# Nine instead of four gate units among the second block's mixers, with room from a smaller descriptor ring, shared masks and a borrowed slot

## The chip, the cores and the metric

The kernel runs on one core of one Trainium2 chip. The metric is device microseconds (us) of one execution. Besides the time, each kernel has one profiled execution, from which every row below is taken. Engines are PE (matrix multiply), DVE (vector), ACT (scalar, tables), POOL (GpSimd) and SP, which issues the weight loads.

## The reference

Two transformer blocks on 256 tokens with a model width of 2048, all in float32. The first block has two mixers (sparse attention, RWKV) and a mixture of experts. The second, which the change is about, is:

```python
proj  = rmsnorm(x, g) @ w_in                    # 2048 -> 12288 columns
gates = sigmoid(proj[..., o_c:].reshape(bsz, seq, 3, 2048) + b_gate)
y_a = gmlp_mixer(proj[..., :2048], ...)         # u * (tril(W) v + b)
y_b = s5_mixer(proj[..., 2048:3072], ...)       # complex diagonal recurrence over time,
                                                # then gelu, then g * sigmoid(g @ w_glu + b)
y_c = stick_breaking_attention(q, k, v)         # 8 heads
br  = einsum('blnw,nwd->blnd', [y_a, y_b, y_c], w_branch)
x = x + sum(gates * br, over the 3 branches) @ w_out
x = x + square(relu(rmsnorm(x) @ w_mlp_in)) @ w_mlp_out
```

## The kernel before

**Weights.** Every dense product is made in two pieces. A 512 KB chunk of weights (`raw`) is loaded by SP, ACT copies its rounded part to `wh` (L213), DVE subtracts to get the rest, `wl` (L214), and PE multiplies both with the activations (L223). One chunk of `w_in` in the second block is 24 matmuls of 256 columns. Both `wh` and `wl` come from a pool of three buffers each, so ACT and DVE can be at most three chunks ahead of PE.

**A gate unit.** `gate` (L1505) makes 256 of the 6144 gate columns: four chunks, so 96 matmuls, four `wh`, four `wl`, then one DVE multiplication by the norm's factors (L1510) and two ACT sigmoids (L1515). There are 24 units. Four of them (`EARLY`) are made among the mixers and kept in the pool `ge`; the other 20 are made one by one in `branch`, each beside the branch product that uses it. Work is the same wherever a unit is made; only its neighbours differ.

**The order in block 2.** `block2` walks `ORDER2`, a list of the dense units: `U` (gMLP), `C` (inputs of S5), `W` (gMLP values), `V` and `Q` (attention), `G` (gate units), `GM`, and `E` (the gelu of S5's output). After each step of a unit a nominal time of PE is added to a count, and each time the count passes `RS`, one step of S5 is written down (`states`: L1989 to L2029). S5 has 32 scans, each a chain on DVE (`a`, L1989 to L1992, and four L2002 scans), then POOL (`b`, `z`, L2004 and L2005; `sl`, L2017), ACT (`sh`) and PE. What the loops write down is then put in order by a scheduler, so that each engine's final order is not the written one.

**Sigmoids.** Their table differs from the ones that the attention heads (`zsb`, `zsc`, up to Exp) and gelu use. So the sigmoids of early units are held back (`held`) until the gelu; one unit's are let go there, the rest in `glu`.

**After the mixers** come `glu` (its input split is `gs`), the `w_branch` products with the remaining gate units, `w_out`, and the MLP.

**Parameter rows.** `late_params` (L449) is called at the start of `moe`, before its slots for weights (`own`, `ring`) are made. It loads 128 rows of 128 parameters by seven DMAs of POOL into a tile, transposes that on PE (L181), and copies the result to `parl`, which the router of the experts needs as `g_ffn` and block 2 as `b_gate` and others. The tile is one of its own, `parl_r`. `cst_c` names the tiles of constants.

Of the kernel before, what the change touches and what calls it, by code (L numbers as in the profile page):

```python
# [10 lines left out]
F32 = mybir.dt.float32  # L11
# [3 lines left out]
OP = mybir.AluOpType  # L15
# [13 lines left out]
def _consts():  # L29
    p = np.arange(128)[:, None]  # L30
    f = np.arange(128)[None, :]
    t = np.arange(T)[None, :]
    c = {}
    c["ident"] = p == f
    c["bd64"] = (p // 64) == (f // 64)
    for d in (128, 64):
        half = d // 2
        inv = np.float32(10000.0) ** (-np.arange(half, dtype=np.float32) * np.float32(2.0 / d))
        ang = np.arange(T, dtype=np.float32)[:, None] * inv.astype(np.float32)[None, :]
        cos = np.cos(ang).astype(np.float32).T  # L40
        sin = np.sin(ang).astype(np.float32).T
        c[f"cos{d}"] = np.tile(cos, (128 // half, 1))
        c[f"sin{d}"] = np.tile(np.concatenate([-sin, sin], 0), (128 // d, 1))
    c["m01"] = np.concatenate([p < 64, p >= 64], 1)
    s, u = p % 64, f[:, :64]
    c["gmask"] = np.concatenate([(s < u) & (p < 64), (s < u) & (p >= 64), s <= u], 1)
    lv = []
    for l in range(6):
        b = 1 << l
        lv.append(((p // (2 * b)) == (f // (2 * b))) & ((p // b) % 2 == 0) & ((f // b) % 2 == 1))  # L50
    c["lev"] = np.concatenate(lv[LB:], 1)
    b = 1 << LB
    c["blk"] = (p // b) == (f // b)
    c["nsel"] = np.where(p % b == f[:, :b], -1.0, 0.0)
    c["iota"] = np.broadcast_to(f, (128, 128))
    c["before"] = p < f
    c["geq"] = p >= f
    c["strict"] = p < f
    c["tril"] = p >= f
    c["ntril"] = np.where(p >= f, -1.0e30, 0.0)  # L60
    c["half"] = (p // 64) == np.arange(2)[None, :]
    c["odd"] = (p // 16) % 2 == np.arange(2)[None, :]
    c["tidx"] = np.broadcast_to(t.astype(np.float32), (128, T))
    return {k: np.ascontiguousarray(v, dtype=np.float32) for k, v in c.items()}
# [3 lines left out]
C1 = ("bd64", "cos128", "sin128", "cos64", "sin64", "m01",  # L68
      "gmask", "lev", "blk", "nsel")
C2 = ("iota", "before")  # L70
C3 = ("geq", "strict", "tril", "ntril", "half", "odd")


def const_arrays():
# [41 lines left out]
class Ker:  # L116
# [47 lines left out]
            return self.mx.tile([128, 512], F32, name="mx", tag="side", bufs=1)  # L164
        return self.mx.tile([128, 512], F32, name="mx", tag="mx", bufs=3)

    def param_rows(self, items, pool, name, q=None):
        nc = self.nc
        n = sum(i[2] for i in items)
        assert n <= 128  # L170
        r = pool.tile([128, 128], F32, name=name + "_r", tag="prow")
        nc.vector.memset(r, 0.0)
        o, where = 0, {}
        for key, parts, cnt in items:
            for ap, r0, c0 in parts:
                rr, cc = ap.shape
                self.tc.keep_in_program_order((q or nc.gpsimd).dma_start(r[o + r0:o + r0 + rr, c0:c0 + cc], ap))
            where[key] = (o, o + cnt)
            o += cnt
        ps = self.pmx()  # L180
        nc.tensor.transpose(ps[:, :128], r, self.ident)  # L181
        p = pool.tile([128, 128], F32, name=name)
        nc.vector.tensor_copy(p, ps[:, :128])
        return {k: p[:, a:b] for k, (a, b) in where.items()}
# [263 lines left out]

    def late_params(self):  # L449

        A = self.A
        row = lambda n: A[n].rearrange("l (r c) -> (l r) c", c=128)
        self.par = self.param_rows([
            ("g_ffn", [(row("g_ffn"), 0, 0)], 16), ("norm1", [(row("norm1_g_2"), 0, 0)], 16),
            ("norm2", [(row("norm2_g_2"), 0, 0)], 16),
            ("b_gate", [(A["b_gate_2"].rearrange("l n (r c) -> (l n r) c", c=128), 0, 0)], 48),
            ("b_glu", [(row("s5_b_glu_2"), 0, 0)], 8), ("s5_d", [(row("s5_d_2"), 0, 0)], 8),
            ("gm_g", [(row("gm_norm_g_2"), 0, 0)], 8)], self.glob, "parl")

    def dump(self, name, t):  # L460
        if name in self.dbg:
# [1017 lines left out]
            later.pop(0)()  # L1479


    EARLY, XB, SB = (4, 2, 1)
    LO, CO = (0, 2)
    PRE = (0,)
    RS, RC = (3.9, 0.52)
    ORDER2 = ('U0', 'C0', 'C1', 'U1', 'U2', 'W0', 'C2', 'C3', 'W1', 'U3', 'GM', 'G0', 'V0', 'Q0', 'Q1', 'V1', 'Q2', 'Q3', 'G1', 'G2', 'E', 'G3')

    def block2(self):
        nc, A, tc = self.nc, self.A, self.tc
        w_in = A["w_in_2"][0]  # L1490
        two = [(0, 128), (128, 128)]
        with ExitStack() as st:
# [130 lines left out]
                    self.split(mh[:, 2 * ci:2 * ci + 2].rearrange("p a t -> p (a t)"),  # L1623
                               ml[:, 2 * ci:2 * ci + 2].rearrange("p a t -> p (a t)"), m)

            self.whole(gate(early, gq, 2, 1))
            glu()
            branch(0, 0, True, False)
            branch(2, 0, False, False)
# [11 lines left out]
    def gmlp(self, y, w_in, vp, chains):  # L1641
        nc, A, c, par = self.nc, self.A, self.c, self.par
        hh, hl = self.hhl
        two = [(0, 128), (128, 128)]
        wsT = vp.tile([128, 8, 128], F32, name="wsT", tag="a")
        bs = vp.tile([128, 8, 128], F32, name="bs", tag="b")
        V = vp.tile([128, 2, 1024], F32, name="gv", tag="V")
        ws = V[:, 0].rearrange("p (g s) -> p g s", g=8)
        vr = self.small.tile([128, 2], F32, name="vr")

        def U(j):
            if j == 0:
                nc.gpsimd.dma_start(ws, A["gm_w_s_2"][0].rearrange("g t s -> t g s"))
                nc.gpsimd.tensor_mul(ws, ws, c["tril"][:, None, :].to_broadcast([128, 8, 128]))
                nc.gpsimd.dma_start(bs, A["gm_b_s_2"][0][None].to_broadcast([128, 8, 128]))
            v, bk = yield from self.ws_steps([(w_in[:, ts(j, 256)], 0)], 256, hh, hl, two)
            yj = y[:, 2 * j:2 * j + 2]
            nc.vector.tensor_mul(yj, bk[0].rearrange("p (a t) -> p a t", a=2), self.row)
            nc.scalar.activation(yj, yj, AF.Gelu_apprx_tanh)
            if j == 1:  # L1660
                for q in range(2):
                    ps = self.pmx()
                    for g in range(4):
                        nc.tensor.transpose(ps[:, ts(g, 128)], ws[:, 4 * q + g], self.ident)
                    nc.scalar.activation(wsT[:, 4 * q:4 * q + 4].rearrange("p g t -> p (g t)"), ps, AF.Copy)

        def W(j):
            banks = yield from self.ts_steps(w_in[:, 1024 + 512 * j:1536 + 512 * j], hh, hl)
            for b in range(2):
                nc.scalar.activation(V[:, b, ts(j, 512)], banks[b], AF.Gelu_apprx_tanh, scale=self.r[:, b:b + 1])  # L1670

        def GM():
            chains.append(mix())
            return
            yield

        def mix():
            vs = self.small.tile([128, 2, 2], F32, name="vs")
            work = vp.tile([128, 768], F32, name="mxd", tag="c")
            for b in range(2):  # L1680
                for j in range(2):
                    self.sumsq(V[:, b, ts(j, 512)], vs[:, b, j:j + 1], work)
            self.rstd(vs, 1024, vr)
            for b in range(2):
                nc.vector.tensor_scalar(V[:, b], V[:, b], vr[:, b:b + 1], None, op0=OP.mult)
            for g in range(8):
                yield
                ps = self.pmx()
                for b in range(2):
                    self.mm(ps[:, ts(b, 128)], V[:, b, ts(g, 128)], wsT[:, g])  # L1690
                mx = work[:, ts(g % 3, T)]
                nc.vector.scalar_tensor_tensor(mx.rearrange("p (b t) -> p b t", b=2),
                                               ps[:, :T].rearrange("p (b t) -> p b t", b=2), par["gm_g"][:, g:g + 1],
                                               bs[:, g][:, None, :].to_broadcast([128, 2, 128]), op0=OP.mult, op1=OP.add)
                nc.vector.tensor_mul(y[:, g], mx, y[:, g])

        steps = {"GM": GM}
        for j in range(4):
            steps[f"U{j}"] = lambda j=j: U(j)
        for j in range(2):  # L1700
            steps[f"W{j}"] = lambda j=j: W(j)
        return steps

    def sb(self, y, w_in, vp, chains):
# [29 lines left out]
        def heads(j, q, k, pre):  # L1734
# [15 lines left out]
            for i, w in enumerate(work):  # L1750
                zs, sp = w[:, 0:384], w[:, 384:768]
                cs = self.pmx()
                self.mm(cs[:, 0:256], c["geq"], sp[:, 0:256], stop=False)
                self.mm(cs[:, 128:256], self.ones, sp[:, 256:384], start=False)
                self.mm(cs[:, 256:384], c["geq"], sp[:, 256:384])
                nc.vector.tensor_sub(zs, zs, cs[:, :384])
                nc.vector.tensor_add(dg(zs), dg(zs), b2(c["ntril"]))
                with self.tc.issue_after(pre):
                    self.lastexp = nc.scalar.activation(zs, zs, AF.Exp).ins
                yield  # L1760
# [411 lines left out]
```

## Time and profile before

| | |
|---|---|
| median of 3 runs | 2948.16 us (2934.23 to 2948.24) |
| the profiled execution's own time | 2951.56 us |
| its span, first to last instruction | 2949.4 us |
| PE busy | 2832.4 us, 96% |
| DVE busy | 2105.3 us, 71% |
| ACT busy | 1612.5 us, 55% |
| POOL busy | 455.1 us, 15%, nearly all of it in S5 |

The shares are means over stages that are limited by different things. Block 2 starts at about 1268 us; the last S5 scan ends at 1745.3 us; `w_branch` runs until about 2140 us.

### The profile page before, as it was taken

How to read it: one execution, taken by the hardware profiler on the slowest of the kernel's cores; microseconds unless marked ns; L12 is line 12 of the kernel's file. 1: busy time of each engine (PE TensorE's matmuls, PEld its weight loads, DVE VectorE, ACT ScalarE, POOL GpSimd, SP SyncE). 2: the span in 40 equal slices, each digit the busy share in tenths (PEclk: the TensorE clock that was granted, in tenths of full speed). 3: DMA queues.
4: the chain of work that ended last, by engine and by line, in shares of the span. 5: the costliest groups of instructions: out<-in, count | busy, mean ns of one | idle time of the engine just before them, and what ended most of it. 6: DMA issues, size and time to landing. Idle time of an engine off the chain costs nothing. (4 is left out here: it accounts for less than half of the span.)

```text
span 2949.4 us, 45262 instructions
## 1 busy us (share of the span) xinstructions
PE 2832.4 (96%) x17284; PEld 2493.9 (85%) x17284; DVE 2105.3 (71%) x2898; ACT 1612.5 (55%) x2161; POOL 455.1 (15%) x623
## 2 busy tenths in 40 slices
PE   8999999997999999998888789999999999999998
PEld 8998989876887788787677789999988888888887
DVE  7685876647998999898999986555555654456554
ACT  6466466536777777765444445444445553345443
POOL 1111111011000000018898840000000000000000
PEclk9999999998999999999999999999999999999999
DMA  6444443484989999864434336666556666666665
GB/s 196 132 118 120 119 118 104 128 285 150 380 296 350 378 379 357 305 176 142 122 115 122 100 110 196 187 187 186 186 186 197 189 188 194 194 189 186 192 193 171
DMA packets 400512, 576.77 MB, mean 196 GB/s; under 512 B 25032, under 2 KB 252624, under 8 KB 400160
## 3 DMA queue, kind: packets, MB, share of 16 engines
q1 hardware_dynamic: 397632, 567.74, 59.6%
q0 software_dynamic: 2624, 6.06, 0.8%
q8 instruction: 137, 2.24, 0.3%
q14 instruction: 87, 0.71, 0.1%
q10 hardware_dynamic: 32, 0.01, 0.0%
HBM read 571.64 MB, written 2.10 MB: 195 GB/s over the span
## 5 line engine op out<-in xcount | busy, mean ns | idle before, releaser
L214 DVE TENSOR_TENSOR wl<-raw,wh 128x1024 fp32r<-128x1024 f32 (+1 forms) x917 | 1133.7, 1241 | 624.5 <-ACT wh L213 604.6
L213 ACT ACTIVATE wh<-raw 128x1024 fp32r<-128x1024 f32 (+1 forms) x917 | 965.2, 1055 | 900.8 <-PE acc L223 686.6
L223 PE MATMUL acc<-hx,wh 128*128 128x256 f32 (+3 forms) x5280 | 1149.8, 306 | 0.5 <-ACT hx L347 0.2
L223 PE MATMUL acc<-hx,wl 128*128 128x256 f32 x3152 | 890.1, 284 | 13.1 <-DVE wl L214 13.0
L223 PEld LDWEIGHTS acc<-hx,wh 128*128 128x128 f32 (+2 forms) x5280 | 849.7, 189 | 55.4 <-issue 8.0
L223 PEld LDWEIGHTS acc<-hx,wl 128*128 128x128 f32 x3152 | 592.8, 188 | 24.1 <-DVE wl L214 15.3
L214 DVE TENSOR_TENSOR wl<-rx,wh 128x1024 fp32r<-128x1024 f32 x159 | 191.3, 1223 | 26.9 <-ACT wh L213 13.6
L223 PE MATMUL acc<-wl,xgh 128*128 128x512 f32 x512 | 201.2, 394 | 2.5 <-DVE wl L214 2.5
L223 PE MATMUL acc<-wh,xgh 128*128 128x512 f32 x512 | 200.1, 391 | 2.9 <-ACT wh L213 2.9
L223 PE MATMUL acc<-wh,xgl 128*128 128x512 f32 x512 | 200.4, 392 | 0.0
L223 PE MATMUL acc<-wh,al 128*128 128x512 f32 x512 | 199.2, 389 | 0.0
L223 PE MATMUL acc<-wh,ah 128*128 128x512 f32 x512 | 199.2, 389 | 0.0
L213 ACT ACTIVATE wh<-rx 128x1024 fp32r<-128x1024 f32 x159 | 167.6, 1061 | 55.9 <-PE acc L223 36.4
L223 PE MATMUL acc<-wl,ah 128*128 128x512 f32 x512 | 179.2, 389 | 0.0
L223 PE MATMUL mx<-wh,act 128*128 128x512 f32 x512 | 140.3, 394 | 1.5 <-DVE act L220 0.8
L223 PE MATMUL acc<-wh,hx 128*128 128x512 f32 x384 | 122.6, 402 | 0.0
L223 PEld LDWEIGHTS acc<-wl,xgh 128*128 128x128 f32 x512 | 96.2, 188 | 25.4 <-DVE wl L214 5.3
L223 PEld LDWEIGHTS mx<-wh,act 128*128 128x128 f32 x512 | 96.6, 189 | 23.2 <-DVE act L220 1.2
L223 PEld LDWEIGHTS acc<-wh,xgh 128*128 128x128 f32 x512 | 96.2, 188 | 23.1 <-ACT wh L213 4.1
L223 PEld LDWEIGHTS acc<-wl,ah 128*128 128x128 f32 x512 | 96.1, 188 | 20.0
L223 PEld LDWEIGHTS acc<-wh,xgl 128*128 128x128 f32 x512 | 96.2, 188 | 19.9
L223 PEld LDWEIGHTS acc<-wh,ah 128*128 128x128 f32 x512 | 96.1, 188 | 19.9
(589 smaller groups left out, 4149.2 us busy)
## 6 DMA issues: line engine op xcount, KB each, us to landing
raw<-in_w_in_dram SPq DMA_DIRECT2D x304, 512.0 KB, 3.7
raw<-in_w_mlp_in_dram SPq DMA_DIRECT2D x128, 512.0 KB, 3.8
raw<-in_w_mlp_out_dram SPq DMA_DIRECT2D x128, 512.0 KB, 3.8
raw<-in_w_e_gate_dram SPq DMA_DIRECT2D x80, 512.0 KB, 6.0
raw<-in_w_e_down_dram SPq DMA_DIRECT2D x77, 512.0 KB, 6.0
raw<-in_w_e_up_dram SPq DMA_DIRECT2D x75, 512.0 KB, 5.7
raw<-in_w_out_dram SPq DMA_DIRECT2D x57, 512.0 KB, 3.8
rx<-in_w_e_up_dram SPq DMA_DIRECT2D x53, 512.0 KB, 6.4
```

The lines of the kernel that those rows point to most:

```text
L213: self.lasth = nc.scalar.activation(h[:, :n], raw[:, :n], AF.Copy).ins
L214: self.lastl = nc.vector.tensor_sub(l[:, :n], raw[:, :n], h[:, :n].bitcast(F32)).ins
L223: return self.nc.tensor.matmul(out, lhsT, rhs, start=start, stop=stop)
```

## The change

Nine gate units run among the mixers in place of four, in a new `ORDER2`; `RS` goes from 3.9 to 4.6, since the nominal time over which S5's steps are spread has grown from 291 to 343 us. The pool `ge` grows by five buffers of 2 KB in each partition. Room for that comes from the ring of DMA descriptors (16384 to 8192 bytes), from two masks (`tril`, equal to `geq`, and `ntril`, now worked out in the same instruction as the addition, L1757), and from the tile `parl_r`: the rows now stand in a weight slot taken by `raw_tile`. The first gate unit after the mixers is then (0, 3).

```diff
-C3 = ("geq", "strict", "tril", "ntril", "half", "odd")
+C3 = ("geq", "strict", "half", "odd")
...
-    def param_rows(self, items, pool, name, q=None):
+    def param_rows(self, items, pool, name, q=None, rows=None):
...
-        r = pool.tile([128, 128], F32, name=name + "_r", tag="prow")
+        r = pool.tile([128, 128], F32, name=name + "_r", tag="prow") if rows is None else rows
...
     def late_params(self):
+        rows = self.raw_tile()[:, :128]
...
-            ("gm_g", [(row("gm_norm_g_2"), 0, 0)], 8)], self.glob, "parl")
+            ("gm_g", [(row("gm_norm_g_2"), 0, 0)], 8)], self.glob, "parl", rows=rows)
...
-    EARLY, XB, SB = (4, 2, 1)
+    EARLY, XB, SB = (9, 2, 1)
-    RS, RC = (3.9, 0.52)
+    RS, RC = (4.6, 0.52)
-    ORDER2 = ('U0', ..., 'GM', 'G0', 'V0', 'Q0', 'Q1', 'V1', 'Q2', 'Q3', 'G1', 'G2', 'E', 'G3')
+    ORDER2 = ('U0', ..., 'GM', 'G0', 'G1', 'V0', 'Q0', 'G2', 'Q1', 'G3',
+              'V1', 'Q2', 'G4', 'Q3', 'G5', 'G6', 'G7', 'E', 'G8')
...
-            self.whole(gate(early, gq, 2, 1))
+            self.whole(gate(early, gq, BR[self.EARLY % 3], self.EARLY // 3))
...
-                nc.gpsimd.tensor_mul(ws, ws, c["tril"][:, None, :].to_broadcast([128, 8, 128]))
+                nc.gpsimd.tensor_mul(ws, ws, c["geq"][:, None, :].to_broadcast([128, 8, 128]))
...
-                nc.vector.tensor_add(dg(zs), dg(zs), b2(c["ntril"]))
+                nc.vector.scalar_tensor_tensor(dg(zs), b2(c["geq"]), -1.0e30, dg(zs), op0=OP.mult, op1=OP.add)
...
-    nc = bacc.Bacc("TRN2", target_bir_lowering=False, num_devices=1)
+    nc = bacc.Bacc("TRN2", target_bir_lowering=False, num_devices=1, dynamic_dma_scratch_size=8192)
```

Three places show what the scheduler made of it. Line numbers of the changed kernel are one to two lower than before's there.

The first is DVE around the last S5 scan, the row `z<-sc,a` that stands last. Before, with three gate multiplications (`g<-acc,row`) ahead of this piece's end and one behind it:

```order
L1992 TENSOR_TENSOR a_18318<-a_18318,a_18319 128x256
L214 TENSOR_TENSOR wl<-raw,wh 128x1024
L1748 TENSOR_TENSOR zsb<-zsb,cst_c_13440 128x2x128
L2002 SCALAR_TENSOR_TENSOR z<-sc,a_18318 128x128 x2
L1510 TENSOR_TENSOR g<-acc,row 128x512
L1747 SCALAR_TENSOR_TENSOR zsc<-zsc 128x384
...
L1756 TENSOR_TENSOR zsb<-zsb,mx 128x384
L2002 SCALAR_TENSOR_TENSOR z<-sc,a_18318 128x128 x2
L1757 TENSOR_TENSOR zsb<-zsb,cst_c_13440 128x2x128
```

The changed kernel, from the last scan on:

```order
L2002 SCALAR_TENSOR_TENSOR z<-sc,a_18834 128x128 x2
L1747 SCALAR_TENSOR_TENSOR zsc<-zsc 128x384
L1748 TENSOR_TENSOR zsb<-zsb,cst_c_13440 128x2x128
L212 TENSOR_TENSOR wl<-raw,wh 128x1024
L1748 TENSOR_TENSOR zsc<-zsc,cst_c_13440 128x2x128
L212 TENSOR_TENSOR wl<-raw,wh 128x1024
L1756 TENSOR_TENSOR zsb<-zsb,mx 128x384
L1757 SCALAR_TENSOR_TENSOR zsb<-cst_c_13440,zsb 128x2x128
L1756 TENSOR_TENSOR zsc<-zsc,mx 128x384
L1510 TENSOR_TENSOR g<-acc,row 128x512
L1757 SCALAR_TENSOR_TENSOR zsc<-cst_c_13440,zsc 128x2x128
L212 TENSOR_TENSOR wl<-raw,wh 128x1024 x3
```

Four instructions of the last pair of heads have moved behind the scan. Four of the five gate multiplications that now stand behind it follow further down, so that five of the nine early units are finished ahead of it.

The second is PE where block 1's `w_out` begins (`acc<-wh,yx`). Before, the transpose of the parameter rows stands far down in it; these are the rows ahead of it and it:

```order
L223 MATMUL acc<-wh,yx 128x512 x4
L223 MATMUL acc<-wl,yx 128x512
L223 MATMUL acc<-wh,yx 128x512 x2
L223 MATMUL acc<-wl,yx 128x512
L181 MATMUL mx<-cst_cg,parl_r 128x128
L1198 MATMUL mx<-cst_cg,xr 128x128 x2
```

And in the changed kernel, from the last matmuls of the attention on:

```order
L221 MATMUL mx<-PT,V 128x128
L221 MATMUL acc<-wh,yx 128x512 x5
L221 MATMUL acc<-wl,yx 128x512
L221 MATMUL acc<-wh,yx 128x512
L221 MATMUL acc<-wl,yx 128x512
L221 MATMUL acc<-wh,yx 128x512
L221 MATMUL acc<-wl,yx 128x512
L221 MATMUL acc<-wh,yx 128x512
L221 MATMUL acc<-wl,yx 128x512
L179 MATMUL mx<-cst_cg,raw 128x128
L221 MATMUL acc<-wh,yx 128x512 x8
```

The transpose has moved up: it stands right behind the first 12 matmuls (one chunk) of `w_out`, ahead of all the others.

The third is ACT around the last gelu of S5's output (`y<-y`) and the sigmoids (`g<-g,parl`). Before:

```order
L213 ACTIVATE wh<-raw 128x1024
L1535 ACTIVATE y_13455<-y_13455 128x512
L1515 ACT_TABLE_LOAD
L1515 ACTIVATE g<-g,parl 128x256 x5
L213 ACTIVATE wh<-raw 128x1024
L1515 ACTIVATE g<-g,parl 128x256 x3
```

And in the changed kernel:

```order
L211 ACTIVATE wh<-raw 128x1024 x2
L1535 ACTIVATE y_13455<-y_13455 128x512
L1515 ACT_TABLE_LOAD
L1515 ACTIVATE g<-g,parl 128x256 x12
L217 ACTIVATE gs<-y_13455 128x512
L1515 ACTIVATE g<-g,parl 128x256 x2
L211 ACTIVATE wh<-raw 128x1024 x4
```

Between two `wh` there now stand 14 sigmoids and a split in place of five sigmoids.

## Rows read from the trace of the kernel before

**Rows 1.** The page: its first line, the span.

```profile
span 2949.4 us, 45262 instructions
```

**Rows 2.** Busy time by stretch, block 2: length, engines (instructions), clock, DMA share, GB/s.

```profile
1340.00:1647.30 307.30, 256.94 (x1598) 222.27 (x1597) 284.91 (x471) 138.22 (x237) 271.33 (x386) 0.96 0.40 119
1647.30:1704.20 56.90, 48.94 (x367) 46.39 (x366) 50.79 (x87) 21.22 (x36) 42.71 (x61) 0.97 0.36 110
1704.20:1745.30 41.10, 32.65 (x223) 30.69 (x222) 40.96 (x67) 14.71 (x23) 23.23 (x16) 0.92 0.31 93
1745.30:1800.00 54.70, 52.91 (x442) 52.30 (x442) 40.73 (x49) 40.59 (x63) 7.33 (x5) 1.00 0.57 173
1800.00:2000.00 200.00, 200.00 (x1701) 200.00 (x1700) 112.99 (x111) 85.74 (x96) 0.00 (x0) 1.00 0.62 187
```

**Rows 3.** Groups by line, DVE, 1340 to 1745.3: busy, mean ns, idle before.

```profile
L214 DVE TENSOR_TENSOR wl<-raw,wh 128x1024 fp32r<-128x1024 f32 x89 | 124.5, 1401 | 8.8 <-ACT wh L213 8.2
```

**Rows 4.** Groups by line, DVE, 1800 to 2000.

```profile
L214 DVE TENSOR_TENSOR wl<-raw,wh 128x1024 fp32r<-128x1024 f32 x71 | 87.0, 1225 | 73.1 <-ACT wh L213 73.1
L1510 DVE TENSOR_TENSOR g<-acc,row 128x512 f32<-128x512 f32 x11 | 7.6, 692 | 6.9 <-PE acc L223 6.9
```

**Rows 5.** What DVE waited for, 1340 to 1745.3: total, times, longest.

```profile
DVE b L2012 <- POOL z L2005: 13.2, 5, 4.2
DVE wl L214 <- ACT wh L213: 8.2, 5, 2.2
```

**Rows 6.** What PE waited for, 1340 to 1745.3.

```profile
PE acc L223 <- DVE wl L214: 18.3, 12, 7.4
```

**Rows 7.** Groups by line, POOL, 1340 to 1745.3.

```profile
L2004 POOL TENSOR_TENSOR b<-z,tab 128x512 f32<-128x512 f32 x31 | 50.7, 1637 | 36.6 <-DVE z L2002 30.1 <-DVE vr L317 3.4 <-DVE vr L314 3.0
```

**Rows 8.** Timeline, DVE, the last attention pair: start, length, instruction, idle before.

```profile
1741.02 1.34 DVE L1747 SCALAR_TENSOR_TENSOR zsc<-zsc 128x384 f32<-128x384 f32 x1
1744.14 0.54 DVE L1756 TENSOR_TENSOR zsb<-zsb,mx 128x384 f32<-128x384 f32 x1
```

**Rows 9.** Timeline, ACT, the last gelu and the first sigmoids.

```profile
1758.16 1.06 ACT L213 ACTIVATE wh<-raw 128x1024 fp32r<-128x1024 f32 x1 [0.53 <-PE acc L223]
1761.47 0.64 ACT L1535 ACTIVATE y<-y 128x512 f32<-128x512 f32 x1 [2.25 <-DVE y L2029]
1763.42 2.11 ACT L1515 ACTIVATE g<-g,parl 128x256 f32<-128x256 f32 x5
1765.43 1.04 ACT L213 ACTIVATE wh<-raw 128x1024 fp32r<-128x1024 f32 x1
```

**Rows 10.** Timeline, PE, behind those sigmoids.

```profile
1767.79 0.39 PE L223 MATMUL acc<-gs,wl 128*128 128x256 f32 x1 [0.76 <-DVE wl L214]
```

**Rows 11.** Timeline, POOL and the tile `parl_r`: parameter rows' DMAs and their landing.

```profile
602.68 0.57 POOL L150 DMA_DIRECT2D cst_c<-in_c_dram  x1 [87.91 <-ACT yx L219]
606.25 0.50 POOL L177 DMA_DIRECT2D parl_r<-in_gm_norm_g_dram  x1
DMA to landing us min/median/max: 5.3/6.1/6.9
```

**Rows 12.** Timeline, SP, loads of `w_out`.

```profile
582.54 0.37 SPq L200 DMA_DIRECT2D raw<-in_w_out_dram  x1
602.18 0.37 SPq L200 DMA_DIRECT2D rx<-in_w_out_dram  x1
```

**Rows 13.** Timeline, PE, where `w_out` of block 1 begins.

```profile
605.37 0.86 PE L223 MATMUL acc<-wh,yx 128*128 128x512 f32 x3
608.17 1.10 PE L223 MATMUL acc<-wh,yx 128*128 128x512 f32 x4
611.59 1.21 PE L223 MATMUL acc<-wh,yx 128*128 128x512 f32 x4 [0.45 <-ACT wh L213]
```

**Rows 14.** Busy time by stretch around the router of the experts.

```profile
612.00:660.00 48.00, 48.00 (x213) 37.35 (x212) 23.67 (x25) 20.33 (x30) 0.01 (x1) 1.00 1.03 361
670.00:690.00 20.00, 4.62 (x21) 4.46 (x22) 12.38 (x39) 7.88 (x14) 7.35 (x5) 0.63 0.02 5
```

More of the change, by code (lines that the diff above doesn't have):

```diff
@@ L58, in _consts @@
     c["strict"] = p < f
-    c["tril"] = p >= f
-    c["ntril"] = np.where(p >= f, -1.0e30, 0.0)
     c["half"] = (p // 64) == np.arange(2)[None, :]
@@ L1479, in experts @@
             later.pop(0)()
-    EARLY, XB, SB = (4, 2, 1)
+    EARLY, XB, SB = (9, 2, 1)
     LO, CO = (0, 2)
     PRE = (0,)
-    RS, RC = (3.9, 0.52)
-    ORDER2 = ('U0', 'C0', 'C1', 'U1', 'U2', 'W0', 'C2', 'C3', 'W1', 'U3', 'GM', 'G0', 'V0', 'Q0', 'Q1', 'V1', 'Q2', 'Q3', 'G1', 'G2', 'E', 'G3')
+    RS, RC = (4.6, 0.52)
+    ORDER2 = ('U0', 'C0', 'C1', 'U1', 'U2', 'W0', 'C2', 'C3', 'W1', 'U3', 'GM', 'G0', 'G1', 'V0', 'Q0', 'G2', 'Q1', 'G3',
+              'V1', 'Q2', 'G4', 'Q3', 'G5', 'G6', 'G7', 'E', 'G8')
     def block2(self):
```

## The prediction

> **What bounds the kernel now.** I first read the span [rows 1]: 2949.4 us, in a profiled execution that took 2951.56 us, 3.4 above the median of 2948.16. The three runs lie 14 us apart, so about 0.5% (14.7 us) is what a measurement of this kernel can tell from no change. PE's 96% over the span says little about the place of the change, so I read the stretches of block 2 [rows 2]. From 1340 to 1745.3, while S5's scans run, DVE is busy for 284.91 + 50.79 + 40.96 = 376.7 of 405.3 us (93%), POOL for 337.3 (83%) and PE for 338.5 (84%). From 1745.3 on it turns round: PE is busy for 52.91 of 54.7 us, then for 200.00 of 200.00, while DVE has 44% idle. So block 2 has two stages with different limits: up to the last scan, DVE; behind it, PE. What moves from the second stage into the first saves PE's time in the second and costs DVE's time in the first. That is the whole of what the change can bring.
>
> Two checks on the first stage. DVE's own waits there are few [rows 5]: 13.2 us for POOL's `z` and 8.2 us for `wh`, of 28.6 idle. And PE's idle time there (405.3 - 338.5 = 66.8 us) is no free room by itself, because its largest such wait, 18.3 us, is for DVE's `wl` [rows 6]: a further chunk needs a further `wl` from the engine that is already the bound.
>
> **What moves, by the order.** Five gate units are 20 chunks. But the scheduler has not put them all ahead of the last scan. Counted over DVE's order from the start of block 2's dense products to the last scan, there are 106 `wl` before and 115 in the changed kernel. Up to the ninth of the 32 scans the two counts are the same, at the 25th they are 90 and 92, at the 29th 99 and 108: most of what moves comes in the last scans. Only 9 of the 20 chunks enter the stage that DVE bounds. The other 11 still stand behind the last scan, where PE bounds, and cost there what they cost in `branch`. The excerpts show it: five gate multiplications of nine stand ahead of the last scan now, three of four before.
>
> **The cost of each part.**
>
> *PE's gain.* 1701 matmuls in 200 us are 0.1176 us each [rows 2], a chunk of 24 is 2.82 us, nine chunks are **-25.4 us** behind the last scan. All of it is gained, for PE has no idle time there.
>
> *DVE's loss.* In the first stage a `wl` takes 1401 ns [rows 3]; where POOL is silent it takes 1225 [rows 4]. Nine are 12.6 us, two more gate multiplications at 692 ns [rows 4] 1.4. Four small instructions of the last attention pair move behind the last scan; two took 1.34 and 0.54 us [rows 8], the other two I put at the smaller, so -3.0. The last scan comes **+11.0 us** later. From below: if the moved work filled the 8.2 us that DVE waited for `wh`, +2.8 would be left. From above: if POOL stood still for each moved `wl` (below), 9 x (1.40 + 1.23) + 1.4 - 3.0 = +22.1. I take the plain sum, because seven of the nine come behind the 25th scan, and in the last 41.1 us of the stage DVE is busy for 40.96 [rows 2]: there is nothing to fill.
>
> A rule of the Trainium skill speaks against the change here. The page "SBUF — State Buffer" (sections "SBUF: two separate sides" and "Who interferes with whom") says that a DVE instruction with two inputs in SBUF and a GpSimd instruction that reads SBUF contend for one pair of ports as a lock, and that the loser stands still for the whole instruction; `wl` has two such inputs. By the rule POOL would lose 1.23 us for each moved `wl`, and the sum would be that of the upper bound. The trace agrees in kind only: 1401 against 1225 ns is 0.18 us of blocking on average, far from whole instructions.
>
> *The last heads.* Those four instructions now stand between the last scan and the Exp of the last heads, and the gelu comes behind Exp. PE has chunks of gate units meanwhile. +1.5 us, between 0 and the 3.0 that moved.
>
> *The sigmoids.* Eight units' sigmoids now wait for the gelu instead of three. Before, ACT made no `wh` from 1759.2 to 1765.43, with five sigmoids of 2.11 / 5 = 0.42 us in it [rows 9], and PE then waited 0.76 us for `wl` [rows 10]. Now 14 sigmoids and a split (0.6, as the gelu's 0.64) stand there: 9 x 0.42 + 0.6 = 4.4 us more. One more `wh` stands ahead of the gelu, which covers up to 2.8 of it, if a buffer is free. **+3**, between 0 and 4.4.
>
> *The borrowed slot.* This lies 1100 us earlier. The DMAs of the parameter rows stand on POOL behind `cst_c`, which waits 87.9 us for the attention's end; the last is issued at 606.25 and such DMAs land 5.3 to 6.9, median 6.1, us after issue [rows 11]: at about 612.4. Before, the transpose stood so far down PE's order that nobody noticed. Now it stands behind the first 12 matmuls of `w_out`, with 216 of its matmuls behind it on PE. Before, those 12 were done when the second chunk began at 605.37, the third at 608.17, the fourth at 611.59 after a wait of 0.45 [rows 13]. Now the second begins at about 612.7, 7.3 later, and the fourth needs no wait any more: **+7**. The slot has another price that lies under this one: the load of `w_out` that went out at 582.54 into that free slot is now the one of 602.18 [rows 12]. If the rows held nobody up, that one chunk's 2.8 us (608.17 - 605.37) would be the loss, and this is the lower bound. The upper: a landing of 6.9 makes +7.7, and PE, idle for 7 us, may come back at the lower of its two clock levels (the granted clock was 0.63 where it was idle for 15 of 20 us [rows 14]), which on three microseconds of work costs another 1.2: 8.9. The shift isn't given back: PE is busy for 48.00 of 48.00 us behind it, and in the router that follows DMA's share is 0.02 [rows 14], so that every weight slot is full and the loads wait for PE too.
>
> *Ring, masks, order at block 2's start.* The mask's addition becomes an instruction with two operations on the same tile: 0. Constants, rows and S5's tables are issued by POOL in another order; one issue is 0.57 us [rows 11], hidden by PE's products before the first scan. I take +0.5, from 0 to 1.1 (two issues). A smaller ring could make POOL wait for descriptors; none of its transfers is needed in the same 10 us, so I cost it at nothing and keep it under that bound.
>
> Sum: -25.4 + 11.0 + 1.5 + 3 + 7 + 0.5 = **-2.4 us**. The profiled execution would be 2949.2, the median 2948.16 - 2.4 = 2945.8: about **2946 us**, no change that can be measured.
>
> **The rivals.** (a) *Two stages, but the first has room.* The moved chunks fill DVE's waits for `wh` (+2.8 instead of 11.0), and the rows land before PE needs them (2.8), with the rest at its lower ends: -25.4 + 2.8 + 2.8 = -19.8, some 2928. For it: 28.6 us of idle DVE and 66.8 of PE in the stage. Against: DVE's full last 41 us, and that more of its waits are for POOL's `z` than for `wh`.
>
> (b) *POOL and DVE lock each other, so it gets slower.* Each moved `wl` delays POOL's `b` and `z` by 1.23 us, and the scan chain, which waits for POOL, with it: the last scan comes 22.1 later and the sum is -2.4 + 11.1 = +8.7, 2957; with the other terms at their upper ends +14.1, 2962. It decides against the change from a last scan 13.4 us later on (25.4 less the 12 of the other terms). For it: POOL's multiplications take 1637 ns [rows 7] and both engines are near full. Against: the mean of `wl` with POOL running, and POOL's own 68 us idle in the stage.
>
> (c) *The units are not earlier in effect*: nothing is gained or lost in block 2, because DVE's later last scan takes all 25.4 and only the seam remains: +7 to +12, 2955 to 2960. This shades into (b).
>
> **How the numbers follow.** The forecast has 0.55, (a) 0.22, (b) with (c) 0.23. The range takes both sets of bounds, 2928 and 2962, and a little for the spread of the runs: 2926 to 2964. Faster by over 0.5% is below 2933.4: most of (a) and a part of the spread, 0.25. Slower by over 0.5% is above 2962.9: the far end of (b), 0.17. Within: 0.58.
>
> **What would show it.** The last scan's start, less the start of block 2, 8 to 14 us later; above 20, the lock is right, below 5, rival (a). PE idle for about 7 us ahead of the transpose at 605 to 613, and the router shifted by as much; without the idle, 3. ACT without a `wh` for about 10 us at the last gelu, and a wait of PE there of 1 to 5. `w_branch` with its five units fewer, 56 us shorter, of which 31 come back ahead of it. The prediction is wrong if S5's steps, not DVE's queue, decide when the last scan comes, or if the nine chunks are not paid on DVE.

## The result, and the profile after

The changed kernel takes **2976.63 us** (median of 4 runs, 2974.37 to 2978.52) against 2947.94 for the one before. The ratio of the means is 1.0108, 95% interval 1.0079 to 1.0138; the ratios below are of the same kind. The forecast was 2946, no change that can be measured, with a range up to 2964. It was wrong: the change costs about 1%.

The page of the changed kernel, first line (before: [rows 1]):

```profile
span 2974.6 us, 45253 instructions
```

The two profiled executions are 25.2 us apart. Where these went is read fastest from four tiles that mark the stages: when the experts' first product starts (`xgh`), when block 2 starts (`hx`), when the last S5 scan starts (`z`), and when the last split of `w_branch` is made (`mh`). In the view of a tile's instructions, the two times are the starts of the first and the last. Before:

```profile
L223 PE MATMUL acc<-wh,xgh x512: 387/389/501, 693.9 to 1247.8; 128*128 128x512 f32 x171
L347 ACT ACTIVATE hx<-mx,parl x32: 455/474/486, 1268.5 to 2238.1; 128x256 fp32r<-128x256 f32 x32
L2002 DVE TENSOR_TENSOR_SCAN z<-sc,a x128: 386/413/1505, 1362.7 to 1744.9; 128x128 f32<-128x128 f32 x128
L219 ACT ACTIVATE mh<-m x8: 632/633/634, 1808.9 to 2142.5; 128x512 fp32r<-128x512 f32 x8
```

And after:

```profile
L221 PE MATMUL acc<-wh,xgh x512: 387/389/501, 724.0 to 1278.0; 128*128 128x512 f32 x171
L345 ACT ACTIVATE hx<-mx,parl x32: 454/473/482, 1297.2 to 2263.3; 128x256 fp32r<-128x256 f32 x32
L2002 DVE TENSOR_TENSOR_SCAN z<-sc,a x128: 389/414/1511, 1392.8 to 1791.4; 128x128 f32<-128x128 f32 x128
L217 ACT ACTIVATE mh<-m x8: 632/633/635, 1890.6 to 2167.6; 128x512 fp32r<-128x512 f32 x8
```

| stage | before | after | difference | forecast |
|---|---|---|---|---|
| start of the span to the experts' first product | 693.9 | 724.0 | +30.1 | +7 |
| from there to block 2 | 574.6 | 573.2 | -1.4 | 0 |
| block 2 to the last scan | 476.4 | 494.2 | +17.8 | +11.5 |
| last scan to the last split | 397.6 | 376.2 | -21.4 | -20.9 |
| from there to the end | 806.9 | 807.0 | +0.1 | 0 |

Block 2, which the change is about, got 3.6 us shorter; the sum had 9.4 (11.5 - 20.9). Its stage behind the last scan came out as forecast, the one ahead of it 6.3 us longer. (`w_branch`, from its first `mh` to its last, went from 333.6 to 277.0 us, 56.6 less; 56 were forecast.) The loss lies in the stage before the experts, where only the borrowed slot was changed. PE's timeline there, behind the first 12 matmuls of `w_out`:

```profile
602.85 0.39 PE L221 MATMUL acc<-wl,yx 128*128 128x512 f32 x1
609.24 0.45 PE L179 MATMUL mx<-cst_cg,raw 128*128 128x128 f32 x1 [6.00 <-DMA raw<-in_gm_norm_g_dram]
633.25 3.78 PE L221 MATMUL acc<-wh,yx 128*128 128x512 f32 x8 [23.57 <-ACT wh L211]
```

Before, the second chunk began at 605.37 [rows 13]. Now there are two stops. The first, 6.00 us, is the forecast one: the transpose waits for the rows' last DMA. The second, 23.57 us, was not seen. PE waits for a `wh`, and ACT's timeline shows what that one waits for:

```profile
632.14 1.06 ACT L211 ACTIVATE wh<-raw 128x1024 fp32r<-128x1024 f32 x1 [31.40 <-DMA raw<-in_w_out_dram]
633.11 1.04 ACT L211 ACTIVATE wh<-rx 128x1024 fp32r<-128x1024 f32 x1
```

ACT takes the chunks in a fixed order, and the next one is in a `raw` slot, not in one of the `rx` slots, whose chunks had been issued from 599.90 on. That `raw` is the borrowed one. SP's order in the changed kernel says why its load is so late (rows left out; the first number is the row's, those behind names are buffers', the brackets say what a row waits for):

```
155 L198 DMA rx_6669<-in_w_out_dram 128x2x512 [waits DMASW3_49,...]
...
171 L198 DMA raw_6674<-in_w_out_dram 128x2x512 [waits DMAHW2_49]
172 L198 DMA raw_6662<-in_w_out_dram 128x2x512 [waits DMASW5_49,DMASW4_49,...,PE_49]
```

The second chunk of `w_out` is `raw_6662`. Before, it was loaded at 582.54 [rows 12], as SP's row 155. Now it may not be loaded until PE has transposed the rows out of its slot, and it stands 17 rows further back, behind 18 other loads of 512 KB, since one of these rows holds two loads. SP's timeline:

```profile
599.90 0.37 SPq L198 DMA_DIRECT2D rx<-in_w_out_dram  x1
600.31 0.46 SPq L393 DMA_DIRECT2D rx<-in_x_dram  x1
600.83 3.66 SPq L198 DMA_DIRECT2D rx<-in_w_out_dram  x6
604.53 2.48 SPq L198 DMA_DIRECT2D raw<-in_w_out_dram  x2
607.65 0.68 SPq L393 DMA_DIRECT2D raw<-in_x_dram  x1
609.08 13.01 SPq L198 DMA_DIRECT2D raw<-in_w_out_dram  x8
634.48 0.37 SPq L198 DMA_DIRECT2D raw<-in_w_e_gate_dram  x1
```

It is the last of the eight that were issued in 609.08 to 622.09, and landed at 632.1. By itself it stands there as

```profile
621.40 0.68 SPq L198 DMA_DIRECT2D raw<-in_w_out_dram  x1
```

So when the transpose had read the rows, its place on SP put it off by another 12 us. Busy time by stretch shows the stop from all sides: no compute engine does anything from 612 to 620 while the DMA engines are full with loads that nobody can use yet.

```profile
605.00:612.00 7.00, 0.45 (x1) 0.18 (x1) 0.46 (x2) 0.00 (x0) 3.51 (x4) 0.51 1.07 354
612.00:620.00 8.00, 0.00 (x0) 0.00 (x0) 0.00 (x0) 0.00 (x0) 0.00 (x0) 0.50 1.06 295
620.00:668.00 48.00, 34.75 (x143) 25.78 (x144) 17.67 (x20) 17.89 (x25) 0.00 (x0) 0.80 0.67 233
```

### The profile page after: what moved, and what is told of

It reads as the page before. It is cut to its first block, busy times and chain, and to the rows that moved or that the text cites. A ratio compares the mean times of both kernels' runs of the same rounds, so it can differ in the third digit from the quotient of the medians.

```text
span 2974.6 us, 45253 instructions
## 1 busy us (share of the span) xinstructions
PE 2841.4 (96%) x17284; PEld 2501.5 (84%) x17284; DVE 2104.5 (71%) x2898; ACT 1611.1 (54%) x2161; POOL 453.6 (15%) x623
## 4 chain that ended last, share of the span: by engine, by line
PE 44%; DVE 7%; POOL 5%; issue 1%; ACT 0%; ACTq 0%; DVEq 0%; POOLq 0%
PE acc L221 42%; DVE wl L212 2%; DVE z L2002 1%; PE mx L221 1%; POOL ttmp L1958 1%; POOL ttmp L1961 1%; POOL tab L1959 1%; POOL z L2005 0%; DVE a L1991 0%; POOL b L2004 0%; DVE a L1990 0%; POOL sl L2017 0%; POOL tab L1957 0%; POOL tab L1962 0%; POOL tab L1960 0%
## 5 line engine op out<-in xcount | busy, mean ns | idle before, releaser
L221 PEld LDWEIGHTS acc<-wh,al 128*128 128x128 f32 x512 | 96.1, 188 | 19.9
```

The costliest lines, as they stand in the source:

```text
L221: return self.nc.tensor.matmul(out, lhsT, rhs, start=start, stop=stop)
```

## The experiments

**Theories.** S: the price of the borrowed slot is the load of its next tenant, which waits for the rows and stands far back on SP. R, the forecast's: only the landing of the rows counts. G: the gates' new order makes the loss. For block 2: D, a chunk moved ahead of the last scan costs its `wl`'s 1.4 us on DVE and saves 2.82 of PE; E, it costs there about what it saves. The median of before was 2948 to 2949 beside each run. The start of block 2 differed by up to 8 us between kernels whose stages ahead of it are nearly the same, so block 2's own length is read from the traces.

**The slot alone** (`b_slot`), in the kernel before:

```diff
+        rows = self.raw_tile()[:, :128]
...
-            ("gm_g", [(row("gm_norm_g_2"), 0, 0)], 8)], self.glob, "parl")
+            ("gm_g", [(row("gm_norm_g_2"), 0, 0)], 8)], self.glob, "parl", rows=rows)
```

> The kernel before with the borrowed weight slot alone (four early gates, old order, old ring, old masks). Theory S, the slot's next tenant: the third weight slot is the next one that w_out's second chunk is loaded into, its load has to wait for the transpose and stands behind 17 others on SP, and ACT's next wh is for it; so PE stands still for about 30 us ahead of the second chunk and the kernel takes 2948 + 28 to 31, some 2977 us. Rival R, as predicted: only the wait for the rows' landing counts, +7, 2955. Rival G, the gates' new order makes the loss: 2948.

2981.57 us, ratio 1.0106 (1.0091 to 1.0122). (The expectation's 17 are SP's rows; they hold 18 loads.) The whole loss, without one gate moved; R and G fall. What PE waited for from 595 to 700 us:

```profile
PE acc L223 <- ACT wh L213: 24.7, 1, 24.7
PE mx L181 <- DMA raw<-in_gm_norm_g_dram: 6.2, 1, 6.2
```

**The changed kernel with its own tile for the rows** (`a_own`), taken from the experts' pool, which is free again when block 2 needs the room:

```diff
-        rows = self.raw_tile()[:, :128]
...
-... self.glob, "parl", rows=rows)
+... self.glob, "parl", rows=p.tile([128, 128], F32, name="parl_r"))
```

> The changed kernel with the rows in a tile of their own in the experts' pool; nine early gates, new order, small ring and shared masks stay. Theory S: the stop of PE at the start of w_out goes, 2976.6 - 29 = 2947, or 2944 with the 3.6 us that the second block got shorter between its first product and its last split of w_branch. Rival R: only 7 come back, 2970. Rival G: no change, 2976.

2950.75 us, ratio 1.0005 (0.9986 to 1.0024). The loss is gone, and nine gates with it are no change against four.

**The slot borrowed, but last in the ring** (`a_ring`):

```diff
-            self.slots, self.nraw = ring + once, -1
+            self.slots, self.nraw = ring[:2] + ring[3:] + once + ring[2:3], -1
```

> The changed kernel, rows still in the borrowed slot, but that slot stands last instead of third in the ring of slots while w_out is loaded. Theory S: w_out's second chunk goes to the next free slot, PE no longer waits for the transpose; the early load of that chunk (582 us) is still lost, some 3 us: 2947 to 2950. Rival R (the landing of the rows is what PE waits for, whatever slot): still +7 over the version with its own tile. Rival G: 2976.

2948.43 us, ratio 0.9998 (0.9988 to 1.0008). The rows' slot is not what is dear, but what comes after them in it. The early load is lost here too, and the 2.8 us that I gave it as a lower bound don't show.

**The slot seventh in the ring** (`a_pos6`):

```diff
-            self.slots, self.nraw = ring + once, -1
+            self.slots, self.nraw = ring[:2] + ring[3:7] + ring[2:3] + ring[7:] + once, -1
```

> The changed kernel, rows in the borrowed slot, that slot now seventh in the ring while w_out is loaded, so that its next tenant is w_out's fifth chunk counted from the stop instead of the second; the load of it stands at SP's row 177 in place of 172, behind 22 others. Theory S, refined (the price is the time from when PE wants the slot's next chunk to when its load lands): PE no longer stops ahead of the transpose, makes three or four chunks more, and then stops for the chunk that lands at about 632 to 640: a stop of some 15 to 25 us at another place, 2965 to 2975. Rival R (the transpose waiting for the rows is the price): none, 2948. Rival L (the slot is dear only because it held the chunk that was loaded early): 2950.

2974.07 us, ratio 1.0090 (1.0061 to 1.0118). PE's timeline: the stop has moved behind the transpose, which no longer waits, and is as dear as before.

```profile
604.71 1.31 PE L221 MATMUL acc<-wh,yx 128*128 128x512 f32 x4 [2.29 <-ACT wh L211]
615.15 0.27 PE L179 MATMUL mx<-cst_cg,raw 128*128 128x128 f32 x1
641.06 2.07 PE L221 MATMUL acc<-wh,yx 128*128 128x512 f32 x4 [22.05 <-ACT wh L211]
```

SP and ACT, the load of that chunk and its `wh`: issued at 629.18, 14 us after the transpose, behind all that SP had ready, and there 10.8 us later.

```profile
629.18 0.38 SPq L198 DMA_DIRECT2D raw<-in_w_out_dram  x1
639.96 1.06 ACT L211 ACTIVATE wh<-raw 128x1024 fp32r<-128x1024 f32 x1 [22.04 <-DMA raw<-in_w_out_dram]
```

That settles S: PE does not wait for the rows here, and the price is the same. It is set by the position of the load on SP, against when its chunk is wanted. Rival L, that only the early load was lost, falls too.

**Everything that makes room, nothing that uses it** (`b_room`): the diff of `a_own`, ring and masks, with `EARLY`, `RS` and `ORDER2` of before.

> The kernel before with all that makes room and nothing that uses it: ring of 8192, masks merged, rows in a tile of the experts' pool; four early gates in the old order. If ring and masks cost nothing: 2948 (within 3). If POOL's loads wait for descriptors or the reordered loads at the second block's start matter: later by 2 to 10, in the stretch between the second block's first product and the first S5 scan. Against the run with its own tile and nine gates this is the pure effect of the five gates: -3.6 by the traces so far, -9 by the prediction's terms.

2951.93 us, ratio 1.0004 (0.9990 to 1.0017). Ring and masks cost nothing that can be measured; block 2 takes 872.5 us from `hx` to `mh`. With 874.0 before and 871.9 in the run with the slot alone, four gates make 872.8 on average; nine with `RS` 4.6 make 870.4, 870.6, 870.3 and 870.9. The five gates bring **2.3 us**, a quarter of the 9.4 in the sum. (These lengths come from the `hx` and `mh` rows of each run's trace, as in the table above.)

**Fewer and more chunks ahead of the last scan**, all on the kernel `a_ring` (`r_` runs) or `a_own` (`o_` runs), by the one number:

```diff
-    RS, RC = (4.6, 0.52)
+    RS, RC = (3.9, 0.52)
```

> The changed kernel with the borrowed slot put last in its ring (as the run of that kind, 2948) and RS 3.9 instead of 4.6: S5's steps come earlier, 110 instead of 115 wl stand ahead of the last scan on DVE. Theory D (a chunk moved ahead of the last scan costs what its wl is busy, 1.4 us of DVE, and saves 2.82 of PE): the last scan 7 earlier, PE's rest 14 longer, 2955. Theory E (in the last four scans PE is as full as DVE, so that a moved chunk costs there about what it saves): within 3 of 2948.

> The same with RS 5.2: 128 wl and eight of the nine gate multiplications ahead of the last scan, S5 drawn out over the gate units from the 24th scan on. Theory D: 13 chunks more, 13 x (2.82 - 1.4) less 2 for the multiplications = -16, 2932. Theory E: within 4 of 2948.

> The same with RS 6.0: 134 wl and all nine gate multiplications ahead of the last scan, and S5 drawn out from the 14th scan on, so that more chunks stand among the scans while PE still waits there. Theory D: 19 chunks more, -27 + 3, 2924. Theory E, with PE's idle time of 38 us between the first and the 24th scan now partly filled: -5 to -10, 2938 to 2943. A third outcome, slower than 2950: S5's end becomes the last thing before glu and PE waits for it.

> The same with RS 4.9: 123 wl and seven gate multiplications ahead of the last scan, between the runs with 115 and 128. Theory E (the second block's time hardly hangs on how many chunks stand ahead of the last scan, as the last scans are full on PE and DVE both): 867 to 871 us for the second block, 2944 to 2949.

> Nine gates, rows in a tile of their own, RS 5.2: 128 wl ahead of the last scan. The same second block as the run with the slot put last and RS 5.2, 867 us from its first product to the last split of w_branch; 2944, and faster than before in the interval. If that run owed its time to the order of the slots: 2950.

| `RS` | `wl` ahead of the last scan | block 2 to last scan | last scan to `mh` | block 2 | median | ratio |
|---|---|---|---|---|---|---|
| 3.9 | 110 | 475.6 | 395.2 | 870.8 | 2949.21 | 0.9999 (0.9989 to 1.0008) |
| 4.6, `a_ring` | 115 | 494.4 | 375.9 | 870.3 | 2948.43 | 0.9998 (0.9988 to 1.0008) |
| 4.9, `o_rs49` | 123 | 516.1 | 353.2 | 869.3 | 2947.44 | 0.9990 (0.9979 to 1.0000) |
| 5.2 | 128 | 523.8 | 343.5 | 867.3 | 2943.69 | 0.9977 (0.9966 to 0.9989) |
| 5.2, `o_rs52` | 128 | 524.0 | 342.3 | 866.3 | 2945.81 | 0.9986 (0.9977 to 0.9995) |
| 6.0 | 134 | 538.3 | 340.4 | 878.7 | 2956.12 | 1.0024 (1.0013 to 1.0036) |

Theory E, and far from D, up to 5.2: 18 chunks more ahead of the last scan shift 50 us from one stage to the other and leave block 2 within 4. At 6.0 E's figure (2938 to 2943) was missed too and the expectation's third outcome came: the last scan was 14.5 later than at 5.2, and only 3.1 were saved behind it. Busy time of that run, from block 2 to the last scan and from there to `mh`; in the second, PE is busy for 326.39 of 340.40:

```profile
1268.60:1806.90 538.30, 481.83 (x3373) 440.94 (x3372) 477.76 (x828) 248.39 (x399) 352.81 (x485) 0.96 0.46 139
1806.90:2147.30 340.40, 326.39 (x2704) 323.79 (x2705) 190.99 (x200) 156.71 (x196) 8.92 (x9) 0.97 0.56 171
```

PE's largest wait in that second stretch is for S5 (`sh`):

```profile
PE mx L221 <- ACT sh L2016: 9.0, 2, 8.4
```

`RS` 5.2 without the late load is faster than the kernel before, by 0.14 and 0.23% in its two versions, and so than the changed one.

**The gates spread over the list** (`r_spread`):

```diff
-    ORDER2 = (..., 'C2', 'C3', 'W1', 'U3', 'GM', 'G0', 'G1', 'V0', 'Q0', 'G2', 'Q1', 'G3',
-              'V1', 'Q2', 'G4', 'Q3', 'G5', 'G6', 'G7', 'E', 'G8')
+    ORDER2 = (..., 'C2', 'G0', 'C3', 'W1', 'G1', 'U3', 'GM', 'G2', 'V0', 'Q0', 'G3', 'Q1', 'G4',
+              'V1', 'G5', 'Q2', 'G6', 'Q3', 'G7', 'E', 'G8')
```

> The same with RS 4.6 as in the changed kernel, but with the gate units spread over the list from C3 on instead of behind GM with five of them at the end: 116 wl ahead of the last scan, yet seven gate multiplications instead of five, and fewer of the chunks in the last four scans (7 instead of 15 between the 28th scan and the last). If what costs is how full the last four scans are, the last scan comes up to 7 us earlier and the time falls to about 2941; if only the number ahead of the last scan counts, 2948.

2955.63 us, ratio 1.0021 (1.0002 to 1.0041), slower than either outcome. The last scan came 497.8 after the start of block 2, later than 494.4, and block 2 took 873.8. But the run does not test the question: from the 28th scan to the last its trace has 15 `wl`, not 7, as many as the changed kernel's, whose row stands first:

```profile
L212 DVE TENSOR_TENSOR wl<-raw,wh x15: 1195/1226/2321, 1732.3 to 1783.5; 128x1024 fp32r<-128x1024 f32 x15
L212 DVE TENSOR_TENSOR wl<-raw,wh x15: 1189/1212/2310, 1706.7 to 1763.2; 128x1024 fp32r<-128x1024 f32 x15
```

Whether fewer chunks in the last four scans would help stays open, and so does why this order is slower.

**A fourth buffer for `wh` and `wl`** (`b_wh4`), in `b_room`:

```diff
-        self.whp = self.pool("wh", 3)
+        self.whp = self.pool("wh", 4)
```

> The run with all that makes room and four early gates in the old order (2952 with 2949 of before beside it), with the room spent otherwise: four instead of three buffers each for wh and wl, 8 KB. Theory W: DVE's time lost in the S5 stage beyond its busy time is its wait for a wh whose buffer PE has not let go; with a fourth buffer DVE's waits for wh there (some 12 us) and PE's for wl (18 to 25) fall to half or less, the second block gets 5 to 12 us shorter, 2940 to 2945. Rival P: wh is late because PE itself is late (full, or waiting for S5), so that a fourth buffer only moves the waits: second block within 2 of 872.5, and 2950.

2957.08 us, ratio 1.0027 (1.0018 to 1.0037), slower, and neither theory as it stood. Block 2 got 5.4 us shorter, 867.1, and PE's wait for `wl` (16.1 us in `b_room`) is no longer among its largest in the S5 stage; but DVE's wait for `wh` stayed, 10.1 against 11.8, and the last scan came no earlier (474.8, 474.9). The stages ahead of block 2 took 8.8 us more in the trace, little beyond the 8 by which such starts differ; why was not followed.

## Why the prediction was wrong, point by point

*The borrowed slot is the step that failed.* It said that the load of 582.54 "is now the one of 602.18", and made the second chunk start at 612.7. The load of 602.18 goes into another slot. The chunk that had been early, the second that PE wants, kept its slot and had to wait for the transpose and for 18 loads. Measured: 6.00 for the rows, about the 7 of the step, and 23.57 for the chunk, which it did not have. `a_pos6` shows that the price is the same when PE does not wait for the rows. A smaller part is the clock. PE stood idle but for the one transpose from 603.24 to 633.25, and then worked for 6 us more at the lower of the two clock levels, 1.2 GHz (granted clock 0.50); by stretch, up to there and behind:

```profile
633.25:639.30 6.05, 6.05 (x14) 4.79 (x15) 4.09 (x4) 3.24 (x3) 0.00 (x0) 0.50 0.51 174
639.30:645.00 5.70, 5.70 (x27) 4.52 (x26) 4.80 (x7) 3.52 (x7) 0.00 (x0) 1.00 0.67 220
```

At the second row's 0.21 us each, the 14 matmuls of the first would have taken 3.0 us: an estimate of some 3 us for the clock. The upper bound had 1.2 for it, which no row gives. Nothing of the shift came back, as forecast: the experts' stage kept its length within 1.4. The step rested on PE's order alone; it is SP's order, and the buffer that ACT's next row names, that hold the price.

*PE's gain.* Right in its mechanism. 223 matmuls, 9.3 chunks, moved ahead of the last scan; behind it the stretch got 21.4 us shorter, against a sum of -25.4, +1.5 and +3, which is -20.9. That it fits so well is in part luck: by the rows below PE's busy time there fell by 23.5, not 25.4, and its idle time rose by 2.1 (1.8 to 3.9), not 4.5. Busy time after, from block 2 to the last scan and from there to `mh`:

```profile
1297.20:1791.40 494.20, 440.17 (x2956) 397.61 (x2955) 453.58 (x797) 226.60 (x375) 349.34 (x488) 0.95 0.42 131
1791.40:2167.60 376.20, 372.29 (x3120) 371.28 (x3121) 220.80 (x230) 178.05 (x220) 10.91 (x6) 0.99 0.57 182
```

And before, the same two stretches:

```profile
1268.50:1744.90 476.40, 407.76 (x2733) 365.52 (x2733) 442.38 (x790) 217.67 (x365) 355.31 (x491) 0.96 0.42 126
1744.90:2142.50 397.60, 395.81 (x3347) 394.87 (x3346) 232.54 (x237) 188.41 (x230) 7.33 (x5) 1.00 0.61 185
```

*The sigmoids and the last heads.* Both waits came, and each within its bounds: +3 and +1.5 were forecast, and from the last scan to 1860 PE waited 2.5 us for `wh` and 3.0 for the heads' `zsb`. Against before they cost less, the 2.1 us of idle time above.

```profile
PE mx L221 <- DVE zsb L1748: 3.0, 1, 3.0
PE acc L221 <- ACT wh L211: 2.5, 2, 2.1
```

*DVE's loss* is the second step that failed, mis-sized as a time though its work was right: DVE's busy time to the last scan rose from 442.4 to 453.6, **+11.2**, the sum had +11.0. But the last scan came 17.8 later, for a forecast of 11.5, and that took most of block 2's gain. The rest is idle time of DVE, 34.0 before and 40.6 after, and it lies in the last four scans. There DVE had been full (40.96 of 41.1 [rows 2]); now PE is the fuller one, 54.13 of 58.9, with 413 matmuls in place of 223, eight chunks more:

```profile
1732.90:1791.80 58.90, 54.13 (x413) 51.72 (x413) 51.42 (x81) 26.21 (x40) 25.41 (x18) 0.97 0.42 135
```

What DVE waited for in it:

```profile
DVE wl L212 <- ACT wh L211: 6.4, 3, 2.9
```

DVE's timeline shows where: the chunks' `wl` stand ahead of S5's next instruction (L1989, at 1754.85), so S5 waits for a weight chunk that ACT has not made.

```profile
1738.60 1.94 DVE L212 TENSOR_TENSOR wl<-raw,wh 128x1024 fp32r<-128x1024 f32 x1 [2.91 <-ACT wh L211]
...
1753.71 1.23 DVE L212 TENSOR_TENSOR wl<-raw,wh 128x1024 fp32r<-128x1024 f32 x1 [2.49 <-ACT wh L211]
1754.85 0.68 DVE L1989 TENSOR_TENSOR a<-mx,tab 128x512 f32<-128x512 f32 x1
```

I had argued that DVE, being full there, would leave nothing to fill; I did not ask what nine more chunks do to PE in the same 41 us. That the two fill up together is what the runs with other `RS` agree with. That ACT's lateness is due to PE is only the trace's reading, from ACT's largest wait in that stretch:

```profile
ACT wh L211 <- PE acc L221: 13.3, 7, 3.1
```

No run isolates it, and the fourth buffer, tried with four gates, hardly shortened DVE's wait.

*The rivals.* (b) was close to the time of the last scan (+22.1 for 17.8), but not by its mechanism: POOL stood idle for 22.55 us ahead of one `b` in that stretch (its row is in the last section). (c), which expected no gain in block 2 and a loss by the slot alone, was nearest (2.3 us of gain), but it took the slot's +7 from the same failed step. (a) did not happen. Ring and masks were rightly put at nothing.

## What to carry to other kernels

Who borrows a buffer must ask three things: what is loaded into it next, when that is wanted, and where that load then stands in its queue. A load that is put off goes behind all that was ready in the meantime; here PE's wait for the borrower itself was 6 us of a stop of 30, and without it the price was the same. A tile of its own in a pool that ends earlier cost nothing that could be measured. And where two engines take turns in being the bound, work moved from one stage to the other is to be added to both engines in the stage that receives it, since the fuller one may change.

## What the runs showed of the hardware

A DVE instruction on one column of 128 values, which takes 0.21 us (the median of its 32), took 1.32 at one place in the changed kernel, the length of the POOL instruction that ran beside it. DVE's timeline:

```profile
1769.39 0.21 DVE L1999 SCALAR_TENSOR_TENSOR a<-z,eh,a 128x1 f32<-128x1 f32 x1
1769.52 1.32 DVE L2000 SCALAR_TENSOR_TENSOR a<-z,eh,a 128x1 f32<-128x1 f32 x1
```

POOL's, at the same time:

```profile
1767.11 2.33 POOL L2004 TENSOR_TENSOR b<-z,tab 128x512 f32<-128x512 f32 x1 [22.55 <-DVE z L2002]
1769.52 1.30 POOL L2005 TENSOR_TENSOR z<-z,tab 128x512 f32<-128x512 f32 x1
```

Such a single instance looks like the whole-instruction blocking that the Trainium skill states ("SBUF — State Buffer", section "Who interferes with whom"); the trace agrees in this one place. I had judged the rule by the mean of `wl` alone, 1401 against 1225 ns. The view of the tile `wl` in the kernel before, 1340 to 1745.3, gives shortest, median and longest:

```profile
L214 DVE TENSOR_TENSOR wl<-raw,wh x89: 1190/1216/2320, 1339.9 to 1742.4; 128x1024 fp32r<-128x1024 f32 x89
```

So the mean hides that at least half are not touched and that the longest takes nearly twice as long. That POOL is what lengthens those is not shown.
